# A hybrid decoder layer on one core: the first branch's output projection as seven half-size products per pair of output blocks, with its sums made earlier

## The chip, the cores and the metric

The kernel runs on one core of one Trainium2 chip. The metric is the device time of one execution in microseconds (us); three executions of a kernel make its median. One profiled execution has a time of its own and a trace. The engines are TensorE (PE, with its weight loads shown apart as PEld), VectorE (DVE), ScalarE (ACT), GpSimd (POOL) and SyncE (SP), whose queue issues the DMA transfers.

## The reference

One layer with two token mixers, x of shape 1024 tokens by 1024 columns, all in float32 (D = 1024):

```
h = RMSNorm(x);  proj = h @ w_in               # all queries, keys, values, gates, merge logits
# branch a: gated linear attention (GLA), 4 heads, dk 128, dv 256, chunks of 64
o_gla = rmsnorm(gla_chunked(q, k, v, log_a), gla_norm_g) * silu(g_gate)
y_a = o_gla @ w_pa                             # "the first branch's output projection"
# branch b: stick-breaking attention, 8 heads, d 128, strictly causal
o_sb = stick_breaking(q, k, v) * silu(s_gate)
y_b = o_sb @ w_pb
g = sigmoid(m_logits + b_gate)                 # one gate per branch and column
x = x + (g_a * y_a + g_b * y_b) @ w_o
return rmsnorm(x) * final_g
```

## The kernel before, in words

**Products.** A float32 matrix product is made of three matmuls: each operand is split into a high part (ACT copies it rounded) and a low part (DVE subtracts the high part), and high x high, high x low and low x high are added in one PSUM bank. `split` does one such pair; its ACT and DVE halves stand at lines 164 and 165. Matmuls have 128 rows of weights and up to 512 columns; T = 1024 tokens are two halves of 512.

**The seven-product form.** The big projections work on pairs of blocks: two blocks of 128 output columns by two halves of tokens, with the 1024 inner rows in two interleaved sets (even and odd blocks of 128). The four quarter matrices on each side, A11 to A22 and B11 to B22, are replaced by seven products of half-size operands, which need sums of quarters: S1 to S4 of the activations and T1 to T4 of the weights. One product is 4 inner blocks x 3 = 12 matmuls of 128x512; a direct pair of output blocks takes 8 x 12. `pair_job` does this for the input projection, with units 0 to 6, and three PSUM banks in turn (tag pp; x, y and z are three of its uses). In each job POOL makes the weight sums (lines 243 to 246) and DVE and ACT empty the banks (lines 275 and 308).

**Stages**, by the profile's time: norm and first values to 103 us; 31 pair jobs from 103 to 770; stick-breaking attention from 770 to 990; the rest of branch a's projection to 1015; branch b's and the output projection, both in the seven-product form, to the end.

Beside the pair jobs other work is placed by hand: `djobs` (decay factors of GLA, the first 25 units), `tjobs` (T sums of w_pb and w_o on DVE, line 839, loaded and stored by DMA), and then the GLA recurrence, 32 steps of (head h, block b of 128 tokens), each with four units of pair jobs: `gl_local` and `gl_out` make the attention of a block, `gl_gate` transposes the normed output of the step before, multiplies it by its gate g (line 973), splits the result and stores it as high and low parts in `d_ogl`. In `gl_out`, r = 1/rms goes DVE - POOL (line 230) - DVE (line 963).

The stick-breaking stage has 64 steps of (head h, block i): `scores` (matmuls z, sigmoid on ACT, a scan on DVE, line 1074), `turn` (transposes on PE, line 1086, splits by ACT and DVE into ath, atl, afh, afl) and per half head `values` (matmuls av, lines 1107 to 1109, then a multiply on DVE, line 1112, and a store to `d_osb`, line 1114). PE gets filler units between them: `st = Line(line)` is a list of loads and units, and `st.run(n)` does the next n units with the loads ahead of them. `SB_PLAN` says how many units stand at each step. The filler is four last gate products and branch a's output projection: `pa(eb, n)`, one output block of 128 columns by one half of the tokens, 24 matmuls (`proj_t`, lines 203 to 205), whose result is multiplied by the merge gate (`ma_half`, line 1162) and stored in `d_ma`.

After the stage, branch b starts: `a_load` brings the stored attention outputs (line 1258), `o_split` splits them (`o_hi` on ACT, line 1306, `o_lo` on DVE, line 1310), and the first products go to tile xa (line 1361). The last units of the filler are placed between these splits. From here on the instructions of ACT, DVE and PE keep the order of the code in the region under `manual_schedule`; elsewhere a scheduler orders them.

## Time and profile before

| | |
|---|---|
| median of 3 executions | 1176.99 us (1176.26 to 1654.08) |
| profiled execution, its own time | 1176.68 us |
| its span in the trace | 1175.0 us |
| PE busy | 1162.1 us, 99% |
| weight loads (PEld) busy | 979.5 us, 83% |
| DVE busy | 857.2 us, 73% |
| ACT busy | 558.3 us, 48% |
| POOL busy | 244.3 us, 21% |
| memory read / written | 150.06 MB / 88.08 MB |

Busy time is the union of an engine's instructions; the span runs from the first to the last event of the trace. Groups of instructions are written as "line engine operation out<-in", with the program's names of tiles. A DVE row "f<-pp,f" reads PSUM bank pp and tile f and writes f. An entry such as [2.00 <-DMA A<-d_osb] behind a row is the time for which the engine stood idle ahead of it and what ended that time.

### The profile page before, as it was taken

The page shows a single profiled execution, that of the slowest core. Times are in us where ns is not written, and L with a number is a line of the kernel's source. Part 1 is how long each engine was busy: PE and PEld are TensorE (multiplying, and loading weights), DVE is VectorE, ACT ScalarE, POOL GpSimd, SP SyncE. Part 2 cuts the span into 40 slices and gives each one's busy share as a digit, 9 for nine tenths or more (in the row PEclk, how much of TensorE's full clock was granted, in tenths as well). Part 3 has the DMA queues.
Part 4 walks back from the last instruction along what each step waited for, and adds up shares of the span by engine and source line. Part 5 has one row for each costly group of instructions (what it writes and reads, how often), then busy time and mean ns, then how long its engine had stood idle before and what let it go on. Part 6 is the DMA issues. An engine that isn't in the chain of part 4 may idle for free.

```text
span 1175.0 us, 16650 instructions
## 1 busy us (share of the span) xinstructions
PE 1162.1 (99%) x5823; PEld 979.5 (83%) x5823; DVE 857.2 (73%) x1441; ACT 558.3 (48%) x1046; POOL 244.3 (21%) x217
## 2 busy tenths in 40 slices
PE   8999999999999999999999999999999999999997
PEld 8999888887888888888888888888888888888886
DVE  6797667888676876776666677457677876488986
ACT  6556663433444545544444343344444444365544
POOL 1022232334242242342242233000000000700001
PEclk9999999999999999999999999999999999999999
DMA  8325549997455665654444357799766656858652
GB/s 290 127 63 162 206 165 327 329 308 241 134 185 180 195 217 162 201 178 133 159 141 131 109 174 237 260 311 337 250 200 216 205 167 195 284 162 286 215 197 108
DMA packets 189456, 239.25 MB, mean 204 GB/s; under 512 B 12438, under 2 KB 128300, under 8 KB 187836
## 3 DMA queue, kind: packets, MB, share of 16 engines
q1 hardware_dynamic: 188796, 237.20, 61.1%
...
q14 instruction: 38, 0.31, 0.1%
HBM read 150.06 MB, written 88.08 MB: 203 GB/s over the span
## 4 chain that ended last, share of the span: by engine, by line
PE 96%; DVE 2%; DMA 1%; ACT 1%; issue 1%; SPq 0%; POOLq 0%; POOL 0%; ACTq 0%; DVEq 0%
PE pp L269 17%; PE pp L270 17%; PE pp L271 17%; PE pp L204 3%; PE pp L205 3%; PE pp L203 3%; PE pp L222 2%; PE av L1108 2%; PE av L1109 2%; PE tr L1086 1%; PE av L1107 1%; PE z L1068 1%; PE z L1070 1%; PE z L1069 1%; PE xa L1363 1%; PE xa L1362 1%
## 5 line engine op out<-in xcount | busy, mean ns | idle before, releaser
L269 PE MATMUL pp<-S,wh 128*128 128x512 f32 x372 | 147.0, 395 | 0.7 <-ACT f L275 0.7
L271 PE MATMUL pp<-S,wl 128*128 128x512 f32 x372 | 145.0, 390 | 0.0
L270 PE MATMUL pp<-S,wh 128*128 128x512 f32 x372 | 144.9, 390 | 0.0
L308 DVE TENSOR_TENSOR f<-pp,f 128x512 f32<-128x512 f32 x93 | 63.9, 687 | 70.2 <-PE pp L271 63.8
L165 DVE TENSOR_TENSOR wl<-tt,wh 128x1024 fp32r<-128x1024 f32 x62 | 75.8, 1222 | 52.6 <-ACT wh L164 52.3
L164 ACT ACTIVATE wh<-tt 128x1024 fp32r<-128x1024 f32 x62 | 65.6, 1059 | 75.0 <-PE pp L270 67.4
L243 POOL TENSOR_TENSOR tt<-raw 128x512 f32<-128x512 f32 x31 | 43.5, 1403 | 258.8 <-DVE wl L165 232.8
L275 ACT ACTIVATE f<-pp 128x512 f32<-128x512 f32 x93 | 55.0, 592 | 79.8 <-PE pp L271 74.2
L1074 DVE TENSOR_TENSOR_SCAN be<-be,m 128x128 f32<-128x128 f32 (+3 forms) x64 | 86.1, 1347 | 3.4 <-ACT be L1071 3.2
L164 ACT ACTIVATE wh<-raw 128x1024 fp32r<-128x1024 f32 (+1 forms) x47 | 48.4, 1030 | 84.0 <-PE pp L270 48.5
L269 PEld LDWEIGHTS pp<-S,wh 128*128 128x128 f32 x372 | 70.5, 190 | 15.1 <-ACT f L275 0.9
L271 PEld LDWEIGHTS pp<-S,wl 128*128 128x128 f32 x372 | 69.8, 188 | 14.8
L270 PEld LDWEIGHTS pp<-S,wh 128*128 128x128 f32 x372 | 69.9, 188 | 13.8
L165 DVE TENSOR_TENSOR wl<-raw,wh 128x1024 fp32r<-128x1024 f32 (+1 forms) x47 | 63.1, 1343 | 18.4 <-ACT wh L164 17.2
L1071 ACT ACTIVATE be<-z 128x384 f32<-128x384 f32 (+4 forms) x96 | 47.2, 494 | 42.7 <-PE z L1070 38.2
L230 POOL TENSOR_TENSOR r<-r,nhalf 128x1 f32<-128x1 f32 x40 | 25.2, 629 | 194.3 <-DVE r L229 194.3
L1268 POOL TENSOR_TENSOR N<-A,A 128x512 f32<-128x512 f32 x4 | 6.6, 1660 | 241.0 <-DMA A<-d_osb 241.0
L269 PE MATMUL pp<-ha11h,wh 128*128 128x512 f32 x124 | 49.2, 397 | 0.0
L269 PE MATMUL pp<-ha12h,wh 128*128 128x512 f32 x124 | 49.0, 395 | 0.0
L164 ACT ACTIVATE dh<-raw 128x512 fp32r<-128x512 f32 x31 | 19.6, 631 | 61.4 <-PE pp L270 61.4
L269 PE MATMUL pp<-ha22h,wh 128*128 128x512 f32 x124 | 48.7, 393 | 0.0
L269 PE MATMUL pp<-S,dh 128*128 128x512 f32 x124 | 48.6, 392 | 0.0
...
## 6 DMA issues: line engine op xcount, KB each, us to landing
...
```

The costliest lines, as they stand in the source:

```text
L164: nc.scalar.activation(hi, src, AF.Copy)
L165: eng.tensor_sub(lo, src, hi.bitcast(F32))
L203: nc.tensor.matmul(pt, whi[:, kb], h_, start=kb == 0, stop=False)
L204: nc.tensor.matmul(pt, whi[:, kb], l_, start=False, stop=False)
L243: nc.gpsimd.tensor_sub(t1, b[:, 0, 1], b[:, 0, 0])
L269: nc.tensor.matmul(pt, bh[:, j], ah[:, j], start=first and j == 0, stop=False, skip_group_check=True)
L270: nc.tensor.matmul(pt, bh[:, j], al[:, j], start=False, stop=False, skip_group_check=True)
L271: nc.tensor.matmul(pt, bl[:, j], ah[:, j], start=False, stop=j == 3, skip_group_check=True)
L275: nc.scalar.activation(t[nm], t[bank], AF.Copy)
L308: nc.vector.tensor_add(add, bank, add)
L1071: nc.scalar.activation(om[:, off + pc * w:off + (pc + 1) * w], zt[:, 0:w], AF.Sigmoid, scale=-inv_sqrt)
L1074: nc.vector.tensor_tensor_scan(rest, rest, m1[:, off:T][:, ::-1], 1.0, op0=ALU.mult, op1=ALU.max)
```

## The change

Branch a's output projection takes the seven-product form. For each of 4 pairs of output blocks, i = 0 to 3, there are seven products of 12 matmuls: 28 x 12 = 336 in place of 16 x 24 = 384. They are grouped into units: A(i) with A11 B11 and S2 T2, B(i) with A12 B21, C(i) with S1 T1 and S4 B22, and D with S3 T3 and then A22 T4 for two values of i, added to one bank. A, B and C are filler of the stick-breaking stage; D is done after it. Between units, partial results u and w are kept in memory (`d_u`, `d_w`).

The sums are made earlier. The T sums of w_pa are made on DVE beside the decays (`tp_load`, `tp_sum`, `tp_store`, into `d_tp`). The S sums of the GLA output are made in `gl_gate`: for b < 4 (the first half of the tokens) the gated block is also stored in `d_g0`; for b >= 4 it is loaded again as gp, POOL makes four 128x128 sums of g and gp, and two more splits and two stores put them into `d_os`. g and gp are loaded in the middle of a step (`gl_g`) instead of two steps ahead. The mask tri moves to another tile. The tail is written in another order: `o_split("bA11")` ahead of the first unit instead of behind it, under `manual_schedule` from there on.

```diff
-SB_PLAN = [0, 0, 0, 1, 0, 0, 1, 0]
+PA_PLAN = {**{(h, 6): 2 if h == 5 else 1 for h in range(8)}, **{(h, 3): 1 for h in (0, 1, 2, 4, 6)}}
...
+    TSUMS = ((0, 1, 0), (1, 3, 1), (3, 3, 0), (2, 2, 3))
+    def tp_load(j):
+        tp[j] = dq.tile([P, 4, HALF], F32, tag="tp", name="tp")
+        for two in range(2):
+            rows = slice((2 * j + two) * P, (2 * j + two + 1) * P)
+            for e in range(2):
+                nc.sync.dma_start(tp[j][:, 2 * two + e].rearrange("p (i c) -> p i c", c=P),
+                                  w_pa[rows].rearrange("p (i e c) -> p e i c", e=2, c=P)[:, e])
+    def tp_sum(j, i):
+        dst, x1, x2_ = TSUMS[i]
+        nc.vector.tensor_sub(tp[j][:, dst], tp[j][:, x1], tp[j][:, x2_])
+    def tp_store(j):
+        nc.sync.dma_start(d_tp[:, j], tp.pop(j))
...
+    for j, (load_at, *sums_at, store_at) in enumerate(((0, 3, 4, 5), (6, 8, 10, 11), (12, 15, 17, 18), (19, 22, 23, 24))):
...
-    for jobs in djobs:
+    for k, jobs in enumerate(djobs):
         pairs.run(1, *jobs)
+        for fn, args in pjobs.get(k, ()):
+            fn(*args)
...
-    tri = gv.tile([P, P], F32, tag="tri", name="tri", bufs=1)
+    tri = const.tile([P, P], F32, tag="rcode", name="tri")
...
-        g = gv.tile([P, 2, P], F32, tag="g", name="g", bufs=3)
-        nc.sync.dma_start(g, d_gg[h][:, :, b * P:(b + 1) * P])
+    def gl_g(h, b):
+        for nm, src, b_ in (("g", d_gg, b), ("gp", d_g0, b - 4))[:1 + b // 4]:
+            g = gblk[h, b][nm] = gv.tile([P, 2, P], F32, tag="g", name="g", bufs=4)
+            nc.sync.dma_start(g, src[h][:, :, b_ * P:(b_ + 1) * P])
...
+        if b < 4:
+            nc.sync.dma_start(d_g0[h][:, :, b * P:(b + 1) * P], t["g"])
+            return
+        g, gp = t["g"], t["gp"]
+        for dst, x1, x2_, fn in ((g[:, 1], g[:, 0], g[:, 1], ALU.add), (g[:, 0], gp[:, 0], g[:, 0], ALU.subtract),
+                                 (gp[:, 0], g[:, 1], gp[:, 0], ALU.subtract),
+                                 (gp[:, 1], gp[:, 1], gp[:, 0], ALU.subtract)):
+            nc.gpsimd.tensor_tensor(dst, x1, x2_, op=fn)
+        o = stage().rearrange("p e (s c) -> p e s c", c=P)
+        for i, src in enumerate((g, gp)):
+            split(src, *(o[:, e, 2 * i:2 * i + 2] for e in range(2)))
+        for e in range(2):
+            nc.sync.dma_start(d_os[:, :, e, h, (b - 4) * P:(b - 3) * P], o[:, e].bitcast(F32))
...
-        pairs.run(4)
+        pairs.run(2)
+        gl_g(h, b)
+        pairs.run(2)
...
+    def pa_mm(a, b, i, pt=None):
...
+        for j in range(4):
+            nc.tensor.matmul(pt, bh[:, j, cs], ah[:, j], start=first and j == 0, stop=False, skip_group_check=True)
+            nc.tensor.matmul(pt, bh[:, j, cs], al[:, j], start=False, stop=False, skip_group_check=True)
+            nc.tensor.matmul(pt, bl[:, j, cs], ah[:, j], start=False, stop=j == 3, skip_group_check=True)
+        return pt
+    def out_put(J, n, i, pt, add, gate_, res):
+        eb = 2 * i + J
+        tc.keep_in_program_order(nc.scalar.activation(gate_, gate_, AF.Sigmoid, bias=vcol[:, eb:eb + 1]))
+        nc.vector.tensor_add(res, pt, add)
+        nc.vector.tensor_mul(res, res, gate_)
+        nc.sync.dma_start(d_ma[eb][:, half(n)], res)
+    def pa_a(i):
+        pt = pa_mm("A11", "B11", i)
+        ps1[i] = f_tile()
+        nc.scalar.activation(ps1[i], pt, AF.Copy)
+        pt, u = pa_mm("S2", "T2", i), f_tile()
+        nc.vector.tensor_add(u, pt, ps1[i])
+        nc.sync.dma_start(d_u[i][:], u)
...
+    def pa_d(i0, J):
+        for i in (i0, i0 + 1):
+            d = pd[i]
+            if J:
+                d["pt"] = pa_mm("S3", "T3", i)
+            else:
+                pa_mm("A22", "T4", i, d["pt"])
+            out_put(J, 1, i, d["pt"], d["wu"[1 - J]], d["o"][:, J], d["wu"[1 - J]])
...
+            C[0], o_dma("A22"), C[1], wload("B22", 1), wload("T3", 0), C[2], C[3], wload("T4", 0),
+            wload("T3", 1), pd_load(0), pd_load(1)]
...
+    wlast = wq_dma("T4", 1, wlast)
+    st = Line([unit_of(pa_d, 0, 1), (lambda: wq_split("T4", 1, wlast), False), pd_load(2), unit_of(pa_d, 0, 0),
+               pd_load(3), unit_of(pa_d, 2, 1), unit_of(pa_d, 2, 0)])
...
+    manual = ExitStack()
+    manual.enter_context(tc.manual_schedule(engines={mybir.EngineType.Activation, mybir.EngineType.DVE,
+                                                     mybir.EngineType.PE}))
+    o_split("bA11", ALL)
     st.run(1)
-    o_split("bA11", ALL)
     o_split("bB11", AB)
...
     sums("b", range(3), ("S1", "S3", "S2"), nc.gpsimd)
-    st.run(1)
     o_load("bT2", "tt")
```

**Order in the recurrence.** POOL's queue at one step with b >= 4 (r is the rms chain, tt the weight sums of a pair job, q2 a part of the next queries), before:

```order
L230 TENSOR_TENSOR r_4598<-r_4598,nhalf_196 128x1
L230 TENSOR_TENSOR r_4743<-r_4743,nhalf_196 128x1
L896 TENSOR_TENSOR q2_5147<-qe_5146,fac_4606 128x512
L243 TENSOR_TENSOR tt_4546<-raw_4544 128x512
L245 TENSOR_TENSOR tt_4546<-raw_4544 128x512
L244 TENSOR_TENSOR tt_4546<-raw_4544,tt_4546 128x512
L246 TENSOR_TENSOR tt_4546<-raw_4544,tt_4546 128x512
```

and with the change, at the same step (g_4632 and g_4634 are g and gp):

```order
L234 TENSOR_TENSOR r_4710<-r_4710,nhalf_210 128x1
L1020 TENSOR_TENSOR g_4632<-g_4632 128x128
L1020 TENSOR_TENSOR g_4632<-g_4634,g_4632 128x128
L234 TENSOR_TENSOR r_4868<-r_4868,nhalf_210 128x1
L1020 TENSOR_TENSOR g_4634<-g_4632,g_4634 128x128
L1020 TENSOR_TENSOR g_4634<-g_4634 128x128
L926 TENSOR_TENSOR q2_5307<-qe_5306,fac_4716 128x512
```

Two sums stand ahead of that step's r, and two behind it. DVE's queue there, before (on is the normed output, asl and the others the splits of the next step):

```order
L229 TENSOR_SCALAR r_4743<-ssq_4741 128x1
L919 TENSOR_TENSOR am1_2639<-pa_4751,tri_2635 64x64
L920 TENSOR_TENSOR am1_2639<-pa_4751,tri_2635 128x64
L963 TENSOR_SCALAR on_4740<-po_4728,r_4743 128x256
L165 TENSOR_TENSOR asl_4757<-am1_2639,ash_4756 128x128
L165 TENSOR_TENSOR vl_4761<-vr_4602,vh_4760 128x256
L165 TENSOR_TENSOR qsl_4765<-q2_4039,qsh_4764 128x128
L165 TENSOR_TENSOR dl_4769<-raw_4347,dh_4768 128x512
```

and with the change:

```order
L233 TENSOR_SCALAR r_4868<-ssq_4866 128x1
L953 TENSOR_TENSOR am1_2693<-pa_4874,tri_2689 64x64
L954 TENSOR_TENSOR am1_2693<-pa_4874,tri_2689 128x64
L997 TENSOR_SCALAR on_4865<-po_4853,r_4868 128x256
L169 TENSOR_TENSOR o_4842<-g_4632,o_4842 128x256
L169 TENSOR_TENSOR o_4842<-g_4634,o_4842 128x256
L169 TENSOR_TENSOR asl_4880<-am1_2693,ash_4879 128x128
L169 TENSOR_TENSOR vl_4884<-vr_4714,vh_4883 128x256
```

Two 128x256 splits of the sums stand between on and asl.

**Order on SP around the last attention values.** d_osb_115 is the store of the last values, A the loads of stored attention outputs, of which the first four are A11; before:

```order
L1155 DMA o<-d_ga_144 128x512
L1258 DMA A_9935<-d_osb_108 128x512
L1258 DMA A_9937<-d_osb_110 128x512
L1114 DMA d_osb_115<-f 128x512
L1258 DMA A_9939<-d_osb_112 128x512
L1258 DMA A_9941<-d_osb_114 128x512
L1258 DMA A_9948<-d_osb_109 128x512
```

and with the change:

```order
L1224 DMA wlast<-d_tp 128x4x256
L1163 DMA d_osb_115<-f 128x512
L1396 DMA A_10284<-d_osb_108 128x512
L1396 DMA A_10286<-d_osb_110 128x512
L1396 DMA A_10288<-d_osb_112 128x512
L1396 DMA A_10290<-d_osb_114 128x512
L1396 DMA A_10297<-d_osb_109 128x512
```

The two A11 loads that stood ahead of the store now stand behind it, and the load of wlast stands there.

**Order on DVE and PE from there.** DVE's queue from the last values on (line 1112, now 1161), before:

```order
L1112 SCALAR_TENSOR_TENSOR f<-av,vend,f 128x128 x4
L1310 TENSOR_TENSOR bB11l<-raw,bB11h 128x1024 x2
L1162 TENSOR_TENSOR o<-pp,o 128x512
L1310 TENSOR_TENSOR bA11l<-A_9935,bA11h 128x512
L1310 TENSOR_TENSOR bA11l<-A_9937,bA11h 128x512
L1310 TENSOR_TENSOR bA11l<-A_9939,bA11h 128x512
L1310 TENSOR_TENSOR bA11l<-A_9941,bA11h 128x512
L1310 TENSOR_TENSOR bA12l<-A_9948,bA12h 128x512
```

and with the change (L1275 and L1276 are the two DVE instructions of `out_put`):

```order
L1161 SCALAR_TENSOR_TENSOR f<-av,vend,f 128x128 x4
L1448 TENSOR_TENSOR bA11l<-A_10284,bA11h 128x512
L1448 TENSOR_TENSOR bA11l<-A_10286,bA11h 128x512
L1448 TENSOR_TENSOR bA11l<-A_10288,bA11h 128x512
L1448 TENSOR_TENSOR bA11l<-A_10290,bA11h 128x512
L1275 TENSOR_TENSOR f<-pp,f 128x512
L1276 TENSOR_TENSOR f<-f,o 128x512
L1275 TENSOR_TENSOR f<-pp,f 128x512
```

All four low halves of A11 stand ahead of the first instruction that empties a bank. PE's queue from the last matmul of the values on, with the change (three rows of one inner block read the high and low parts; pp_10329 is the bank of D for i = 0):

```order
L1158 MATMUL av_10239<-ath_7978,v_9775 128x256
L1254 MATMUL pp_10346<-oa22h_8850,wh_9833 128x512
L1255 MATMUL pp_10346<-oa22l_8851,wh_9833 128x512
L1256 MATMUL pp_10346<-oa22h_8850,wl_9834 128x512
L1254 MATMUL pp_10346<-oa22h_8850,wh_9833 128x512
L1255 MATMUL pp_10346<-oa22l_8851,wh_9833 128x512
L1256 MATMUL pp_10346<-oa22h_8850,wl_9834 128x512
L1254 MATMUL pp_10346<-oa22h_8850,wh_9833 128x512
L1255 MATMUL pp_10346<-oa22l_8851,wh_9833 128x512
L1256 MATMUL pp_10346<-oa22h_8850,wl_9834 128x512
L1254 MATMUL pp_10329<-oa21h_9657,wh_10187 128x512
L1255 MATMUL pp_10329<-oa21l_9658,wh_10187 128x512
```

The rows on pp_10346 are the last nine matmuls of S3 T3. The first on pp_10329 is that of A22 T4, which adds to the bank that L1275 reads first. Before, PE had 112 matmuls of `pa` between the values and the first on xa; it now has 81.

More of the change, by code (lines that the diff above doesn't have):

```diff
@@ L1195, in hybrid_layer, with wq_dma @@
-    for eb in range(5):
-        line += ([pa(eb, 0)] if eb > 2 else []) + [pa(eb, 1), pa_load(eb + 3)]
-    line += [pa(eb, n) for n in range(2) for eb in range(5, KB)]
+    wo = {}
+    def wq_dma(nm, ii, raw):
+        raw = raw.rearrange("p k c -> p (k c)").rearrange("p (j c) -> p j c", j=4)
+        if nm[0] == "T":
+            nc.sync.dma_start(raw, d_tp[:, :, ("T1", "T3", "T4", "T2").index(nm), ii * DV:(ii + 1) * DV])
+        else:
+            e, J = int(nm[1]) - 1, int(nm[2]) - 1
+            rows = w_pa.rearrange("(j e p) c -> e p j c", e=2, p=P)[e]
+            for i in range(2):
+                c0 = (2 * (2 * ii + i) + J) * P
+                nc.sync.dma_start(raw[:, :, i * P:(i + 1) * P], rows[:, :, c0:c0 + P])
+        return raw
@@ L1212, in hybrid_layer @@
             scores(*steps[s + 2])
-        st.run(SB_PLAN[i] if i == 6 or h in (0, 1, 2, 4, 6) else 0)
+        st.run(PA_PLAN.get((h, i), 0))
         turn(h, i)
@@ L1341, in hybrid_layer @@
     o_load("bT3")
-    st.run()
+    st.run(1)
     def part_of(w, j, cols):
```

102 lines of the change are left out of this document (73 added, 29 removed).

## The prediction

> **What bounds the kernel now.** I read the page first (share of each engine, then the chain of work that ended last), then the waits of TensorE (PE), then the stages one by one.
>
> ```profile
> PE 1162.1 (99%) x5823; PEld 979.5 (83%) x5823; DVE 857.2 (73%) x1441; ACT 558.3 (48%) x1046; POOL 244.3 (21%) x217
> PE 96%; DVE 2%; DMA 1%; ACT 1%; issue 1%; SPq 0%; POOLq 0%; POOL 0%; ACTq 0%; DVEq 0%
> ```
>
> PE is busy 99% of 1175.0 us and carries 96% of the chain. The waits of PE (line, what it waited for, us in total, times, longest) say the same: only start-up costs over 1 us.
>
> ```profile
> PE warm L148 <- POOL ident masks.py:199: 1.4, 1, 1.4
> PE pp L222 <- DVE vw L499: 1.3, 1, 1.3
> PE pp L269 <- ACT f L275: 0.7, 1, 0.7
> ```
>
> So a removed matmul is worth its full step as long as nothing else comes late, and a wait that is added on PE counts in full. The step has to be read with care: a row gives 0.39 to 0.40 us, but matmuls overlap. Here are the last matmul of the attention values (its end, 990.05, is called T below), the first two filler matmuls behind it, and the first of the second branch.
>
> ```profile
> 989.77 0.28 PE L1109 MATMUL av<-ath,v 128*128 128x256 f32 x1
> 989.89 0.40 PE L205 MATMUL pp<-oa11h,wl 128*128 128x512 f32 x1
> 990.12 0.40 PE L203 MATMUL pp<-oa12h,wh 128*128 128x512 f32 x1
> 1015.30 0.39 PE L1361 MATMUL xa<-bA11h,bB11h 128*128 128x512 f32 x1
> ```
>
> 112 matmuls stand between the values and the second branch, and (1015.30 - 989.89) / 112 = 0.227 us a step.
>
> **The change part by part.** (1) *Removed matmuls.* The projection had 16 products of 24 matmuls, 384; it now has 4 pairs of 7 products of 12, 336. 48 x 0.227 = **-10.9 us**. By the row's 0.39 it would be -18.7, which no step from start to start supports. In program order 17 of the 48 go before T (-3.9) and 31 after it: the tail goes from 112 to 81 matmuls.
>
> (2) *A new wait in the tail.* Splitting the second branch's A11 used to stand behind a filler unit and now stands before the next one. The rows of SyncE's queue (SPq), ACT and DVE around T:
>
> ```profile
> 988.41 0.91 SPq L1258 DMA_DIRECT2D A<-d_osb  x2
> 991.24 0.32 SPq L1114 DMA_DIRECT2D d_osb<-f  x1
> 991.61 8.10 SPq L1258 DMA_DIRECT2D A<-d_osb  x12
> 995.38 0.63 ACT L1306 ACTIVATE bA11h<-A 128x512 fp32r<-128x512 f32 x1 [2.00 <-DMA A<-d_osb]
> 996.24 0.63 ACT L1306 ACTIVATE bA11h<-A 128x512 fp32r<-128x512 f32 x1 [0.23 <-DMA A<-d_osb]
> 990.09 1.12 DVE L1112 SCALAR_TENSOR_TENSOR f<-av,vend,f 128x128 f32<-128x128 f32 x4 [5.00 <-PE av L1109]
> 993.74 0.69 DVE L1162 TENSOR_TENSOR o<-pp,o 128x512 f32<-128x512 f32 x1 [0.26 <-PE pp L205]
> 996.90 0.69 DVE L1310 TENSOR_TENSOR bA11l<-A,bA11h 128x512 fp32r<-128x512 f32 x1 [0.17 <-ACT bA11h L1306]
> ```
>
> Before, two of the four A11 loads went out at 988.4, ahead of the store that waits for the last values; the other two left from 991.61 and were split at 995.38 and 996.24, while PE had products to go on with. Now all four stand behind that store, so the first leaves at about 991.6, is split from about 995.4, and the fourth comes three spacings later: 3 x 0.45 by the issue (0.91 for two) or 3 x 0.86 by the arrivals (996.24 - 995.38), so 996.7 to 998.0. Add 0.63 on ACT and 0.69 on DVE for the low half, and 0.69 for the eviction that is queued right behind it on DVE: 998.7 to 1000.0. That eviction empties the bank to which PE's tenth matmul after T adds. PE has nine matmuls until then, 9 x 0.227 = 2.0 us, to 992.1. It then stands for 6.6 to 7.9 us; I take **+7.2**. The tail so has 81 x 0.227 = 18.4 of work and 7.2 of waiting, 25.6 against 25.4 before: its gain is gone. What is behind is covered: until it has emptied the next bank, DVE has three 128x1024 splits (wlast, bB11) and four evictions to do, 3 x 1.23 + 4 x 0.69 = 6.5 us by the rows of term 4, and PE has 36 matmuls (8.2 us) to go on with.
>
> (3) *The clock after that wait.* Windows at the end of the span (PE, weight loads, DVE, ACT, POOL busy, granted clock, DMA):
>
> ```profile
> 1167.65 0.28 PE L1490 MATMUL pp<-wT4h,A22l 128*128 128x256 f32 x1
> 1170.00:1171.00 1.00, 0.00 (x0) 0.00 (x0) 0.56 (x2) 0.30 (x1) 0.66 (x1) 1.00 0.40 154
> 1171.00:1172.00 1.00, 0.00 (x0) 0.00 (x0) 0.25 (x1) 0.31 (x1) 0.00 (x0) 0.59 0.00 0
> 1172.00:1173.00 1.00, 0.00 (x0) 0.00 (x0) 0.00 (x0) 0.00 (x0) 0.00 (x0) 0.50 0.89 344
> ```
>
> PE's last matmul ends at 1167.93, and the granted clock falls to 0.50 between 1171 and 1172, about 3.3 us later. A stall of 7 us is longer than that, so PE should resume at half clock. How long it stays there no row of before shows: at least 0, at most all 72 matmuls left, which would lose another 16.3. I take as long as the fall needed, 3.3 us at half speed, which loses 1.65: **+1.7**. The Trainium skill, "TensorE: Matmul & The Clock Gate", section "What's actually happening", gives about 3.4 us of activity until the full clock returns; an estimate by it is a loss of 1.7, and no run here shows it yet.
>
> (4) *More work on DVE in the stick-breaking stage.* Between its first scan and T, DVE gets 13 more filler evictions (26 for 13) and 5 more weight splits (12 for 7).
>
> ```profile
> 770.00:990.00 220.00, 219.53 (x1210) 186.93 (x1209) 161.29 (x242) 102.77 (x218) 0.00 (x0) 1.00 0.70 233
> L165 DVE TENSOR_TENSOR wl<-raw,wh 128x1024 fp32r<-128x1024 f32 x7 | 8.6, 1226 | 6.6 <-ACT wh L164 6.0
> L1162 DVE TENSOR_TENSOR o<-pp,o 128x512 f32<-128x512 f32 x11 | 7.6, 692 | 28.2 <-issue 16.1 <-PE pp L205 12.1
> PEld tr L1086 <- DVE atl L165: 5.6, 17, 0.5
> ```
>
> That is 13 x 0.69 + 5 x 1.23 = 15.1 us on an engine that had 220 - 161.3 = 58.7 free, so on average it is covered, and PE loses only 3.9 us of cover. But weight loads of the transposes already wait 17 times for a DVE split, 5.6 us in all. Between 0 and 15.1 I take **+1.0**, near the lower end, because the free time is four times the addition.
>
> (5) *The recurrence.* In 16 of its 32 steps POOL makes four 128x128 sums, two of them ahead of r, for which DVE waits; DVE and ACT then split two more 128x256 tiles. POOL rows of 128x128 don't exist: they lie between r (128x1) and 128x512, 0.55 to 1.3.
>
> ```profile
> 503.29 0.55 POOL L230 TENSOR_TENSOR r<-r,nhalf 128x1 f32<-128x1 f32 x1
> 389.24 1.29 POOL L243 TENSOR_TENSOR tt<-raw 128x512 f32<-128x512 f32 x1 [3.32 <-DVE wl L165]
> 386.56 0.42 DVE L165 TENSOR_TENSOR vl<-vr,vh 128x256 fp32r<-128x256 f32 x1
> 501.00 1.19 DVE L165 TENSOR_TENSOR vl<-vr,vh 128x256 fp32r<-128x256 f32 x1
> 503.88 0.48 DVE L963 TENSOR_SCALAR on<-po,r 128x256 f32<-128x256 f32 x1 [1.69 <-POOL r L230]
> 513.55 0.39 PE L269 MATMUL pp<-S,dh 128*128 128x512 f32 x1
> 514.67 0.68 DVE L308 TENSOR_TENSOR f<-pp,f 128x512 f32<-128x512 f32 x1
> 516.27 0.39 PE L269 MATMUL pp<-ha22h,wh 128*128 128x512 f32 x1
> L308 DVE TENSOR_TENSOR f<-pp,f 128x512 f32<-128x512 f32 x54 | 37.2, 688 | 46.2 <-PE pp L271 43.5 <-issue 2.7
> ```
>
> What PE needs is the eviction L308: the bank whose product ends as the next one begins (513.55) must be empty by 516.27, one product of 12 x 0.227 = 2.7 us later. If DVE comes at once, 2.7 - 0.7 = 2.0 us are to spare; at 514.67 it came 1.1 after that and 0.9 were left. Added per step on DVE: 2 x 0.42 of splits, and up to 1.1 to 2.6 of waiting behind two sums. Against that DVE idles 46.2 / 54 = 0.86 us ahead of each eviction. Between nothing and 16 x 1.1 = 18 I take **+2.0**, an overrun of 0.1 a step on average, nearest to the 503.88 row, where 1.69 of waiting for POOL cost PE nothing.
> The Trainium skill, "SBUF — State Buffer", section "Who interferes with whom", speaks against this part: a DVE instruction with two SBUF inputs contends with a GpSimd instruction that reads SBUF. The trace agrees in one pair above: the same 128x256 split took 0.42 alone and 1.19 while POOL made sums.
>
> (6) *Sums beside the decays.* 16 more tensor_sub of 128x512 and 8 MB of transfers:
>
> ```profile
> 200.00:300.00 100.00, 99.31 (x443) 81.39 (x442) 81.19 (x109) 38.19 (x57) 34.42 (x26) 1.00 0.86 285
> L839 DVE TENSOR_TENSOR t<-t x32: 678/692/1783, 190.5 to 270.0; 128x512 f32<-128x512 f32 x32
> ```
>
> 32 such sums (median 0.692 each) in a stretch with DVE at 81% and DMA at 0.86 left PE 99.3 of 100. The new 16 x 0.69 = 11.1 us come earlier, beside the decays. Between 0 and 11.1 I take **+0.4**.
>
> **Sum.** -10.9 + 7.2 + 1.7 + 1.0 + 2.0 + 0.4 = +1.4. Against the profiled run of 1176.68 (span 1175.0 and 1.7 around it; the median 1176.99 is 0.3 higher) that gives **1178**.
>
> **Rivals.** *No stall in the tail.* If the A11 data come early, or PE doesn't wait for that eviction, terms 2 and 3 go: 1178 - 8.9 = 1169. For it: before, the same splits cost PE nothing. Against it: the order on SP, DVE and PE. Chance 0.13. *DVE becomes the bound in the stick-breaking stage.* With half of the 15.1 us on the path, 1178 - 1.0 + 7.5 = 1184.5. For it: 5.6 us of waits for atl already; against it: 58.7 us free. Chance 0.14. *The recurrence goes slower (the other side).* If the contention of the pair 0.42 and 1.19 holds for the new splits, they cost 2 x 1.19 = 2.4 a step, and with two sums of 0.55 to 1.29 ahead of r DVE is 3.5 to 5.0 late. It decides once the delay passes the 2.0 to spare; the overrun of 1.5 to 3.0 in 16 steps is 24 to 48 us, and with 2.0 taken out of the sum the time is 1200 to 1224. For it: the 0.9 left at 514.67. Against it: the 0.86 of idle time ahead of each eviction. Chance 0.07.
>
> **How the numbers follow.** My forecast has 0.66, by itself 1173 to 1183 (stall 6.6 to 7.9, clock 0 to 3.3, the other terms up to twice their value). The range of 1167 to 1189 takes in the first two rivals and leaves out the third and the far ends of terms 3 to 5. Two per cent is 23.5 us, about what a measurement can tell from no change. Faster by that needs under 1153.5, beyond the 10.9 that the matmuls can give: 0.01. Slower needs over 1200.5, the third rival: 0.07. The rest, 0.92, is within.
>
> **What would show it.** Right: 48 matmuls of L205's kind fewer; one PE wait of about 7 us on a DVE eviction some 2 us after the last values, a granted clock of 0.50 behind it, and the second branch starting 25 to 28 us after T; T itself no more than 4 us earlier, minus what terms 4 to 6 take. Wrong: a tail under 20 us, many PE waits on atl, or on L308's evictions in the 16 steps with sums.

## The result: 1205.87 us, 2.5% slower, and the profile after

The median of six executions of the changed kernel is 1205.87 us (1205.05 to 1208.23), against 1177.02 for the kernel before: a ratio of 1.0248, interval 1.0234 to 1.0262. One of the six executions of the kernel before took 1654.08 us; the ratio is of the fast executions alone. The profiled execution has a span of 1203.1 us, 28.1 more than before. The first thing to read is again the share of PE and the chain of work that ended last.

```profile
PE 1158.9 (96%) x5775; PEld 972.1 (81%) x5775; DVE 915.6 (76%) x1519; ACT 576.0 (48%) x1088; POOL 282.2 (23%) x281
PE 72%; issue 6%; DMA 6%; POOL 6%; DVE 6%; ACT 2%; SPq 1%; POOLq 0%; DVEq 0%; ACTq 0%
```

The 48 matmuls are gone (5823 to 5775). But PE, which carried 96% of the chain, now carries 72%; POOL, DMA and DVE have 6% each. The work became less, and the waiting became more. The waits of PE in the whole span (line, what it waited for, us in total, times, longest) name the places:

```profile
PE pp L1254 <- DVE f L1275: 15.3, 2, 11.1
PE pp L273 <- DVE f L312: 4.9, 6, 1.7
PE pp L273 <- ACT f L279: 3.7, 2, 2.2
```

L1254 is the projection's own matmul in the tail, L273 that of the pair jobs; L1275, L312 and L279 empty banks. A list of waits shows neither a slow clock nor many short delays. So I also worked out an **excess** from the start times of all matmul rows: for each neighbouring pair, the time from start to start beyond the usual step of its shape (0.227 us for 512 columns), summed by stage.

| excess of PE, us | before | after | difference |
|---|---|---|---|
| start (to 100 us) | 8.6 | 8.6 | 0.0 |
| decays and T sums of w_pa (100 to 280) | 0.2 | 5.8 | +5.6 |
| recurrence and the other pair jobs (280 to the first z) | 17.7 | 26.4 | +8.7 |
| stick-breaking stage (first z to T) | 11.8 | 16.4 | +4.6 |
| tail and rest (from T) | 0.1 | 19.7 | +19.6 |
| sum | 38.4 | 76.9 | +38.5 |

38.5 - 10.9 for the removed matmuls is 27.6, against 28.1 in the span: the table accounts for the loss. T itself comes 15.0 us later (1005.0 for 990.05; -3.9 + 5.6 + 8.7 + 4.6 = 15.0), and xa starts 37.8 after T where it started 25.3 after.

**The tail.** Rows of the timelines of SP, ACT, DVE and PE from T on (start, duration, engine, line, operation, tiles, count, and in brackets the idle time ahead and what ended it):

```profile
1004.73 0.28 PE L1158 MATMUL av<-ath,v 128*128 128x256 f32 x1
1005.93 0.53 SPq L1224 DMA_DIRECT2D wlast<-d_tp  x1
1007.16 10.66 SPq L1396 DMA_DIRECT2D A<-d_osb  x14
1014.20 2.58 ACT L1444 ACTIVATE bA11h<-A 128x512 fp32r<-128x512 f32 x4 [16.46 <-DMA A<-d_osb]
1014.87 2.64 DVE L1448 TENSOR_TENSOR bA11l<-A,bA11h 128x512 fp32r<-128x512 f32 x4 [8.68 <-ACT bA11h L1444]
1017.42 0.68 DVE L1275 TENSOR_TENSOR f<-pp,f 128x512 f32<-128x512 f32 x1
1018.16 0.79 PE L1254 MATMUL pp<-oa21h,wh 128*128 128x512 f32 x1 [11.08 <-DVE f L1275]
1028.15 6.82 DVE L1448 TENSOR_TENSOR bA12l<-A,bA12h 128x512 fp32r<-128x512 f32 x4
1034.89 0.68 DVE L1275 TENSOR_TENSOR f<-pp,f 128x512 f32<-128x512 f32 x1
1035.71 0.47 PE L1254 MATMUL pp<-oa21h,wh 128*128 128x512 f32 x1 [4.25 <-DVE f L1275]
```

The predicted stall is there: A11 is loaded, split on ACT and DVE, then the bank is emptied, then PE goes on. It lasts 11.08 where 6.6 to 7.9 was forecast, because the data land 7.0 us after the first load's issue (1007.16 to 1014.20, by the start of the split on ACT); before it was 3.8 (991.61 to 995.38). And there is a second stall of 4.25: four splits of A12 take 6.82 us on DVE, 1.7 each, and stand ahead of the third unit's eviction. Before, the same split took 0.63:

```profile
1000.64 1.89 DVE L1310 TENSOR_TENSOR bA12l<-A,bA12h 128x512 fp32r<-128x512 f32 x3
1027.63 1.74 POOL L1406 TENSOR_TENSOR A<-N,A 128x512 f32<-128x512 f32 x1
```

The second row, of the kernel after, is what runs beside them now: POOL's S sums of branch b.

What stands ahead of A11 on SP, in before (the first two rows) and after (the last three):

```profile
976.21 1.89 SPq L1284 DMA_DIRECT2D raw<-in_w_pb_dram  x3
980.95 1.48 SPq L1278 DMA_DIRECT2D tt<-d_t  x3
997.73 1.22 SPq L1422 DMA_DIRECT2D raw<-in_w_pb_dram  x2
1002.62 2.13 SPq L1422 DMA_DIRECT2D raw<-in_w_pb_dram  x3
1004.86 1.03 SPq L1416 DMA_DIRECT2D tt<-d_t  x2
```

Before, these loads of branch b's weights and of its T sums had all been issued by 983.4, 5 us ahead of the first A11 load. Now five loads of weights, two of tt, two of gates and the 512 KB of wlast, 2.75 MB in all, leave in the 9 us before A11. As I read it, the filler's weight splits hold the load buffers longer: the last of them ahead of these loads ends on DVE at 997.63, and the first two loads leave at 997.73.

**The clock.** Windows of the tail (us; busy time of PE, weight loads, DVE, ACT and POOL; granted clock; DMA share; GB/s):

```profile
1008.00:1010.00 2.00, 0.00 (x0) 0.00 (x0) 0.00 (x0) 0.00 (x0) 0.00 (x0) 0.76 0.73 235
1010.00:1012.00 2.00, 0.00 (x0) 0.00 (x0) 0.00 (x0) 0.00 (x0) 0.00 (x0) 0.50 1.03 357
1020.00:1022.00 2.00, 2.00 (x6) 1.58 (x5) 2.00 (x3) 2.00 (x4) 0.22 (x1) 0.50 1.05 394
1022.00:1024.00 2.00, 2.00 (x8) 1.57 (x8) 2.00 (x2) 2.00 (x5) 1.92 (x2) 0.83 1.03 382
1036.00:1038.00 2.00, 2.00 (x7) 1.56 (x6) 1.90 (x3) 2.00 (x5) 1.92 (x3) 0.58 0.92 352
```

PE stopped at 1007.08 (1018.16 - 11.08). A mean clock of 0.76 from 1008 to 1010 puts its fall to half at about 1009.0, 2 us later, and it is still half from 1020 to 1022. At the second stall PE stopped at 1031.46 and went on at 1035.71; by the 0.58 of the last window the clock fell only at about 1036.3. By the starts of the matmuls, the step is 0.427 from 1018.16 to 1022.6 (4.4 us) and again, after the second stall, from 1036.26 to 1039.59 (3.3 us). That loses 7.7 x (1 - 0.227 / 0.427) = 3.6 us. 11.1 + 4.25 + 3.6 = 18.95 of the tail's 19.7.

**The recurrence.** One step with sums, on POOL, ACT and PE:

```profile
495.62 1.12 POOL L1020 TENSOR_TENSOR g<-g 128x128 f32<-128x128 f32 x2 [0.70 <-DVE o L169]
497.22 1.20 POOL L1020 TENSOR_TENSOR g<-g 128x128 f32<-128x128 f32 x2
496.77 0.42 ACT L168 ACTIVATE o<-g 128x256 fp32r<-128x256 f32 x1 [0.86 <-POOL g L1020]
498.45 0.42 ACT L168 ACTIVATE o<-g 128x256 fp32r<-128x256 f32 x1 [1.06 <-POOL g L1020]
499.72 0.58 ACT L279 ACTIVATE f<-pp 128x512 f32<-128x512 f32 x1
500.35 0.50 PE L273 MATMUL pp<-S,dh 128*128 128x512 f32 x1 [1.49 <-ACT f L279]
L1020 POOL TENSOR_TENSOR g<-g 128x128 f32<-128x128 f32 x64 | 34.1, 532 | 71.4 <-DVE o L169 64.1
```

A sum of 128x128 takes 0.53 on POOL on average. ACT stands 0.86 and 1.06 for them, since its splits of the sums come next in its line. Behind them in the same line, after one more weight split, stands L279, which empties a bank, and PE waits 1.49 for it.

This isn't one step alone. The groups of these splits over the whole stage, on ACT before (the first row) and after, and on DVE after:

```profile
L164 ACT ACTIVATE o<-g 128x256 fp32r<-128x256 f32 x32 | 13.0, 406 | 1.5 <-DVE g L973 0.7 <-ACT qsh L164 0.5 <-DMA d_k<-o 0.3
L168 ACT ACTIVATE o<-g 128x256 fp32r<-128x256 f32 x64 | 26.3, 412 | 46.2 <-POOL g L1020 40.8 <-DMA d_k<-o 1.9 <-DVE g L1007 1.5
L169 DVE TENSOR_TENSOR o<-g,o 128x256 fp32r<-128x256 f32 x64 | 35.0, 548 | 13.6 <-ACT o L168 13.1
```

ACT stands 46.2 us ahead of them, 40.8 of it for POOL's sums, where it stood 1.5 before; DVE stands 13.6, nearly all for ACT's half of the same split, where it stood 0.4. The splits themselves didn't get longer on DVE: 0.55 on average, for 0.61 before.

**The decays.** DVE and PE at two places:

```profile
153.60 0.69 DVE L831 TENSOR_TENSOR tp<-tp 128x512 f32<-128x512 f32 x1 [1.45 <-DMA tp<-in_w_pa_dram]
158.81 1.39 DVE L831 TENSOR_TENSOR tp<-tp 128x512 f32<-128x512 f32 x2
161.25 0.68 DVE L312 TENSOR_TENSOR f<-pp,f 128x512 f32<-128x512 f32 x1
161.99 0.50 PE L273 MATMUL pp<-ha22h,wh 128*128 128x512 f32 x1 [1.72 <-DVE f L312]
187.78 0.69 DVE L555 SCALAR_TENSOR_TENSOR f<-f 128x512 f32<-128x512 f32 x1 [1.79 <-DMA f<-d_e]
190.98 0.47 PE L273 MATMUL pp<-S,wh 128*128 128x512 f32 x1 [1.50 <-DVE f L555]
```

DVE stands 1.45 for the weights that the new sums read. From there DVE has next to no pause until 161.93. At the end of this stretch two more sums and a weight split stand ahead of an eviction, and PE waits 1.72. And DVE stands 1.79 for a transfer of decay factors (f<-d_e).

### The profile page after: what moved, and what is told of

It is laid out like the page before. It is cut to its first block, busy times and chain, and to the rows that moved or that the text cites. A ratio compares the mean times of both kernels' runs of the same rounds, so it can differ in the third digit from the quotient of the medians.

```text
span 1203.1 us, 17066 instructions
## 1 busy us (share of the span) xinstructions
PE 1158.9 (96%) x5775; PEld 972.1 (81%) x5775; DVE 915.6 (76%) x1519; ACT 576.0 (48%) x1088; POOL 282.2 (23%) x281
## 4 chain that ended last, share of the span: by engine, by line
PE 72%; issue 6%; DMA 6%; POOL 6%; DVE 6%; ACT 2%; SPq 1%; POOLq 0%; DVEq 0%; ACTq 0%
PE pp L273 12%; PE pp L274 12%; PE pp L275 12%; POOL g L1020 2%; PE pp L226 2%; PE pp L1254 1%; PE pp L1255 1%; PE pp L1256 1%; PE av L1156 1%; PE av L1158 1%; PE av L1157 1%; PE xa L1502 1%; PE xa L1501 1%; PE xa L1503 1%; PE xb L1625 1%
## 5 line engine op out<-in xcount | busy, mean ns | idle before, releaser
L273 PE MATMUL pp<-S,wh 128*128 128x512 f32 x372 | 147.4, 396 | 1.5 <-DVE f L555 1.5
L169 DVE TENSOR_TENSOR wl<-tt,wh 128x1024 fp32r<-128x1024 f32 x62 | 76.9, 1240 | 35.1 <-ACT wh L168 34.6
L312 DVE TENSOR_TENSOR f<-pp,f 128x512 f32<-128x512 f32 x93 | 63.7, 686 | 51.1 <-PE pp L275 46.4
L168 ACT ACTIVATE wh<-raw 128x1024 fp32r<-128x1024 f32 (+1 forms) x52 | 53.6, 1031 | 73.4 <-PE pp L274 31.3
L279 ACT ACTIVATE f<-pp 128x512 f32<-128x512 f32 x93 | 54.7, 590 | 65.2 <-PE pp L275 61.6
L169 DVE TENSOR_TENSOR wl<-raw,wh 128x1024 fp32r<-128x1024 f32 (+1 forms) x52 | 71.3, 1372 | 18.0 <-ACT wh L168 15.9
L273 PEld LDWEIGHTS pp<-S,wh 128*128 128x128 f32 x372 | 70.6, 190 | 16.6 <-ACT wh L168 1.9
L275 PEld LDWEIGHTS pp<-S,wl 128*128 128x128 f32 x372 | 69.9, 188 | 14.9
L273 PE MATMUL pp<-ha22h,wh 128*128 128x512 f32 x124 | 49.4, 399 | 4.9 <-DVE f L312 4.9
L273 PE MATMUL pp<-S,dh 128*128 128x512 f32 x124 | 48.9, 394 | 3.7 <-ACT f L279 3.7
L1020 POOL TENSOR_TENSOR g<-g 128x128 f32<-128x128 f32 x64 | 34.1, 532 | 71.4 <-DVE o L169 64.1
L273 PE MATMUL pp<-ha11h,wh 128*128 128x512 f32 x124 | 49.2, 397 | 0.0
L273 PE MATMUL pp<-ha12h,wh 128*128 128x512 f32 x124 | 49.0, 395 | 0.0
```

The costliest lines, as they stand in the source:

```text
L168: nc.scalar.activation(hi, src, AF.Copy)
L169: eng.tensor_sub(lo, src, hi.bitcast(F32))
L273: nc.tensor.matmul(pt, bh[:, j], ah[:, j], start=first and j == 0, stop=False, skip_group_check=True)
L275: nc.tensor.matmul(pt, bl[:, j], ah[:, j], start=False, stop=j == 3, skip_group_check=True)
L279: nc.scalar.activation(t[nm], t[bank], AF.Copy)
L312: nc.vector.tensor_add(add, bank, add)
```

## The experiments

Ratios are to the kernel before, run beside each; "excess" is the table's number for a stage, of the profiled run. No version here is faster than before. The excess of a stage isn't the same in all runs that leave that stage as the change has it: the decays have 4.9 to 7.9 (a wait at the border of 280 us falls to one side or the other), the recurrence 26.4 to 28.2, the stick-breaking stage 15.3 to 16.4 (17.8 in e6) and the tail 19.3 to 21.1. One or two microseconds of excess in a single run therefore show nothing.

Five of the sixteen times (e2, e5, e7, e15, e16) lie where the theory under test put them. e6, e9, e11, e12, e13 and e17 came out slower than anything that was expected of them.

### The tail

**e1_tail**: the units are done earlier, two ahead of the splits of A11 and one more ahead of the splits of B11, so that the evictions of their banks no longer stand behind these.

```diff
+    st.run(1)
+    st.run(1)
     o_split("bA11", ALL)
-    st.run(1)
-    o_split("bB11", AB)
...
+    st.run(1)
+    o_split("bB11", AB)
     sums("b", range(3), ("S1", "S3", "S2"), nc.gpsimd)
...
     o_load("bT1")
-    st.run(1)
     o_split("bB21", AB)
...
     o_load("bT3")
-    st.run(1)
```

> The tail in another order: both products of the first D pair come before the splits of A11, the split of B11 stands between the other two D units, and POOL's sums and the A12 splits come behind. Nothing else differs from the changed kernel (1205.9). Theory 'in line' (evictions queued on DVE behind splits whose data are late): both PE waits (11.1 and 4.25 us) and the half clock behind them (about 3.6 us) go, a new wait of up to 2 us ahead of the second branch: 1187 to 1190. Rival 'the loads are the bound' (the A11 data arrive 9 us after the last values whatever the order, and the second branch can't start earlier): PE only waits elsewhere, ahead of xa, and the time stays at 1202 to 1206.

Measured: 1201.24 us, 1.0208 (1.0193 to 1.0223). The tail's excess goes from 19.7 to 15.3 only. Waits of PE from 1003 us on, and the row of DVE behind the longest:

```profile
PE pp L1254 <- DVE f L1275: 8.2, 2, 6.2
1026.65 0.69 DVE L1275 TENSOR_TENSOR f<-pp,f 128x512 f32<-128x512 f32 x1 [3.82 <-DMA f<-d_w]
```

The eviction isn't behind the splits any more, yet PE waits for the same line: it now needs f<-d_w, the partial result w, whose load stands behind the A loads on SP. One wait has taken the place of another.

**e16_a12_behind**: only the split of A12 is moved behind the third unit.

```diff
-    o_split("bA12", ALL)
     sums("b", [3], ("S1", "S3", "S2"), nc.gpsimd)
     o_load("bT1")
     st.run(1)
+    o_split("bA12", ALL)
```

> The changed kernel with one move: the splits of A12 stand behind the third D unit's evictions instead of ahead of them. Theory 'in line' (the A12 splits, slowed by POOL's sums beside them, hold up the eviction): the second wait of 4.25 us and the half clock behind it (about 1.5 us) go, 1200 to 1202. Rival (the eviction's other operand, w of the third pair, is late too): the wait only changes its cause, 1204 to 1206.

Measured: 1201.09 us, 1.021 (1.0192 to 1.0228). The place of the second stall on PE:

```profile
1036.10 0.50 PE L1254 MATMUL pp<-oa21h,wh 128*128 128x512 f32 x1 [0.82 <-DVE f L1275]
```

The second wait falls from 4.25 to 0.82, the tail's excess from 19.7 to 14.1, and the time by 4.8. So the second stall, with its spell of half clock, is due to the place of these four splits. They are as long at their new place (6.90 us for the four, for 6.82), but no eviction that PE waits for stands behind them.

**e14_no_wpb**: 3 MB of branch b's weights (B11, B21, T2) are not loaded but filled with a constant by POOL; the order on ACT, DVE and PE stays, and A11 keeps its place behind the store.

```diff
+        if nm in ("bB11", "bB21", "bT2"):
+            for j in range(4):
+                nc.gpsimd.memset(raw[:, j], 0.5)
+            return
```

> The changed kernel without the loads of three weight operands of the second branch (bB11, bB21, bT2: twelve of 256 KB around the last values; POOL fills the tiles with a constant in their place, so that part of the computation is left out). The loads of A11 keep their place in the queue, behind the store of the last values. Theory 'bytes ahead': A11 is split 3.4 to 4.5 us after its first issue in place of 7.0, PE's long wait falls from 11.1 to 7 to 8.5 us, the second wait shrinks too: 1196 to 1202. Rival 'place behind the store': the wait stays at 10 to 11.5, 1203 to 1206.

Measured: 1202.64 us, 1.0211 (1.0195 to 1.0228); the tail's excess is 16.7. SP, ACT and PE:

```profile
1005.88 8.11 SPq L1396 DMA_DIRECT2D A<-d_osb  x14
1009.63 0.63 ACT L1448 ACTIVATE bA11h<-A 128x512 fp32r<-128x512 f32 x1 [12.57 <-DMA A<-d_osb]
1014.35 0.80 PE L1254 MATMUL pp<-oa21h,wh 128*128 128x512 f32 x1 [7.96 <-DVE f L1275]
```

Without those transfers A11 lands 3.75 us after its issue, as before the change, and PE waits 7.96. So 8.0 of the 11.1 remain without these transfers, close to the prediction's upper end of 7.9, and the transfers give 3.1. That the 8.0 comes from the place behind the store is the prediction's working and was not tested by itself.

**e10_extra_1mb** tried the reverse: four copies of 256 KB within memory were put ahead of A11.

```diff
     wlast = wq_dma("T4", 1, wlast)
+    for i in range(4):
+        nc.sync.dma_start(d_x[i][:], d_osb[SB_H - 1][:, half(0)])
```

> The changed kernel with 1 MB of additional transfers (four copies of 256 KB from memory to memory, which nobody waits for), issued some 7 us before the last values. Theory 'bytes' (the transfer engines are full around the end of the stick-breaking stage, and A11 lands when what stands ahead of it is done): the long wait of PE grows from 11.1 to 13 to 15 us, 1208 to 1211. Rival 'order and latency' (A11 lands a fixed time after its issue, which the store of the last values sets): 11 to 11.5 us and 1205 to 1207.

Measured: 1205.59 us, 1.0239 (1.0224 to 1.0255), tail's excess 19.2, longest wait 9.5. The time lies where the rival had it, but this is inconclusive. The copies pushed other loads (two of w_pb, two of tt) out of the 9 us ahead of A11, so that again 2.75 MB left there, and the run doesn't add what it was to add.

**e6_tail_need** issues the loads in the order of need: A12 behind the second unit, A21 and A22 behind the third, all sums behind the fourth, and splits wlast only ahead of the last unit.

```diff
-               pd_load(3), unit_of(pa_d, 2, 1), unit_of(pa_d, 2, 0)])
+               pd_load(3), unit_of(pa_d, 2, 1), (lambda: wq_split("T4", 1, wlast), False), unit_of(pa_d, 2, 0)])
...
-    a_load("A12", ALL)
-    a_load("A21", range(3))
-    a_load("A22", range(3))
...
+    st.run(1)
+    st.run(1)
     o_split("bA11", ALL)
+    a_load("A12", ALL)
     st.run(1)
...
```

> The tail with transfers and splits in the order of need: evictions ahead of all splits as in the tail kernel above (1201.2), and besides the loads of A12, A21 and A22 are issued behind the loads of w and u for the last two pairs, and the split of wlast stands only ahead of the unit that uses it. Theory 'late data in line' (the tail waits for wlast, w and u, which stand behind 14 other loads): the waits of 2.0 and 6.2 us that the tail kernel still has go, less 1 to 3 us of new waits for A12 later: 1191 to 1196. Rival 'bytes' (the transfer engines are full in the tail, over 1.0 by the windows, and the sum of bytes sets the start of the second branch): 1199 to 1203.

Measured: 1207.58 us, 1.026 (1.0239 to 1.028), the tail's excess 21.6: no gain.

```profile
PE pp L1501 <- DVE kept L1538: 8.8, 1, 8.8
PE pp L1254 <- ACT wh L168: 5.9, 1, 5.9
```

PE now waits 5.9 for the high half of the last weights, on ACT, and 8.8 in branch b, where POOL's sums come late.

**e11_d_later** loads A11 and B11 ahead of wlast and does branch b's first four products between the second and the third unit, as cover.

```diff
     a_load("A11", ALL)
     o_load("bB11")
+    wlast = mo.tile([P, KB, P], F32, tag="wr", name="wlast")
+    wlast = wq_dma("T4", 1, wlast)
...
+    st.run(2)
     o_split("bA11", ALL)
...
+    for it in items[:4]:
+        a_product(*it)
+    late_tail()
```

> The tail with less in front of A11 and more cover behind it: the loads of A11 are issued ahead of wlast, PE does the first pair of D units at once, then the first four products of the second branch, and only then the other D units, whose data have the 11 us of those products longer to arrive. Theory 'bytes' (the data come at the rate of the transfers, and only other work on PE helps): the tail's PE waiting and half clock of 20 us fall to 6 to 12, 1191 to 1199. Rival (the waits only move again, to the products that need A12 and POOL's sums): 1201 to 1207.

Measured: 1209.21 us, 1.027 (1.0253 to 1.0287), tail's excess 23.5. xa starts 12.4 after T, as meant, but it was no cover:

```profile
PE pp L1503 <- DVE bB21l L1444: 5.6, 1, 5.6
PE xa L1501 <- ACT bB11h L1440: 4.9, 1, 4.9
```

Whichever operand PE is given first, it waits for that one. In the three windows of the changed kernel above that lie between 1010 and 1024, the DMA share is 1.03 to 1.05 at 357 to 394 GB/s. As I read it, all that the tail loads after T competes, and a new order only chooses what is late.

### The recurrence

**e2_gla_nosum** leaves out POOL's four sums; the splits and stores stay. **e3_gla_dve** makes them on DVE. **e7_late_split** leaves them on POOL but does their splits and stores half a step later.

```diff
-            nc.gpsimd.tensor_tensor(dst, x1, x2_, op=fn)
+            nc.vector.tensor_tensor(dst, x1, x2_, op=fn)
```

This is e3; e2 leaves out the whole loop. And e7:

```diff
+        pend.append((g, gp, h, b))
...
+    def gl_flush():
+        while pend:
+            g, gp, h, b = pend.pop()
+            o = stage().rearrange("p e (s c) -> p e s c", c=P)
+            for i, src in enumerate((g, gp)):
+                split(src, *(o[:, e, 2 * i:2 * i + 2] for e in range(2)))
...
         pairs.run(2)
+        gl_flush()
         gl_g(h, b)
```

> The recurrence without the four POOL sums per step: the splits take g and gp as they are (part of the computation left out), all loads, splits and stores stay. Theory 'in line' (ACT and DVE stand in the queue for POOL's sums, and evictions of the pair jobs behind them come late): the stages of the recurrence lose 7 to 9 us of PE waiting, 1197 to 1199. Rival 'more work' (two more splits on ACT and DVE and two more loads and stores per step): nothing comes back, 1204 to 1206.

> The same four sums per step, made on DVE in place of POOL. Theory 'in line': no wait between engines, 4 x 0.28 us more on DVE in 16 steps, which has idle time: PE waits of the recurrence fall from 8.7 to 1 to 3 us, 1198 to 1201. Rival 'more work': DVE has 1.1 us more per step, PE waits more, 1206 to 1215.

> POOL's sums in the recurrence stay, but the splits and stores of their results stand half a step later, so that ACT and DVE find them ready. Theory 'in line' (it is the wait for POOL, not the work of the sums or splits): as without the sums, 1198 to 1200. Rival 'shared memory port' (POOL's sums slow DVE's own splits wherever they stand): 1203 to 1206.

| | time, us | ratio (interval) | excess of the recurrence, us |
|---|---|---|---|
| the change | 1205.87 | 1.0248 (1.0234 to 1.0262) | 26.4 |
| e2, no sums | 1198.3 | 1.0173 (1.0156 to 1.019) | 19.8 |
| e3, sums on DVE | 1201.92 | 1.022 (1.0205 to 1.0235) | 23.5 |
| e7, splits later | 1198.1 | 1.0178 (1.0163 to 1.0193) | 18.3 |

e7 does all the work of the change, with the same sums on POOL, and its recurrence is 8.1 us better, down to 0.6 above the kernel before. That is as much as leaving the sums out brings. So neither the sums nor the splits are too much work; ACT and DVE stood in line for POOL with evictions behind them. In e7 ACT stands 20.8 us for POOL ahead of these splits, for 40.8, and DVE 3.2, for 13.6. DVE's splits are even longer there, 0.63 on average for 0.55, so their length isn't what costs. With the sums on DVE the gain is 2.9: DVE's standing goes as well (1.5), but ACT still stands 13.2 for the sums, and their work is added on DVE.

### The decays

**e5_notp** leaves out the loads, sums and stores of the T sums of w_pa and reads the T sums of w_pb in their place. **e8_tp_late** has the loads of the last three groups one job earlier and the first sums of the second and third group one job later. **e12_late_tppool** makes the sums on POOL, on top of e7.

```diff
-        for fn, args in pjobs.get(k, ()):
-            fn(*args)
```

```diff
-    for j, (load_at, *sums_at, store_at) in enumerate(((0, 3, 4, 5), (6, 8, 10, 11), (12, 15, 17, 18), (19, 22, 23, 24))):
+    for j, (load_at, *sums_at, store_at) in enumerate(((0, 3, 4, 5), (5, 9, 10, 11), (11, 16, 17, 18), (18, 22, 23, 24))):
```

```diff
-        nc.vector.tensor_sub(tp[j][:, dst], tp[j][:, x1], tp[j][:, x2_])
+        nc.gpsimd.tensor_sub(tp[j][:, dst], tp[j][:, x1], tp[j][:, x2_])
```

> Without the sums of w_pa beside the decays: no loads, sums or stores there; the T operands are read from the stored sums of w_pb instead (part of the computation left out). If these sums and their transfers cause all PE waiting between 100 and 300 us (4.5 us in three places): 1201 to 1202. Rival (the pair jobs' new order in that stage causes it): 1205 to 1206.

> The loads of w_pa for the second to fourth group of sums go out one unit earlier and the sums of the second and third stand one unit later. If DVE's wait for these loads is the cause in the stage of the decays: one of the three waits (1.7 us) goes, 1203 to 1205. If the transfers themselves delay the decay factors (the wait of 1.5 on f<-d_e), that wait stays or grows: 1205 to 1207.

> The splits of the recurrence's sums half a step later (as in the kernel of 1198.1) and the sums of w_pa beside the decays on POOL in place of DVE, with the same transfers. If DVE's line (its wait for the w_pa data and three sums ahead of an eviction) is the cause in the decays: the waiting of 5.8 us there falls to 1.5 to 3, 1194 to 1196. If the transfers are (late decay factors): it stays, 1197 to 1200.

e5: 1201.9 us, 1.0215 (1.0194 to 1.0235); the excess of the decays is 0.1, so the T sums and their transfers cost all 5.6 us there. e8: 1205.57, 1.0251 (1.0228 to 1.0274), 6.8: the shift by one job gains nothing. e12: 1214.92, 1.0323 (1.0308 to 1.0339). Its recurrence keeps e7's gain in the main (19.7), but the decays lose 23.0. Waits of PE from 100 to 285 us:

```profile
PE pp L275 <- DVE wl L169: 7.8, 1, 7.8
```

POOL makes the pair jobs' own weight sums; the new ones stand in their line, and PE waits 7.8 at once for a weight split.

### The stick-breaking stage

**e17_mul_pool** moves the 16 gate multiplications of `out_put` from DVE to POOL, to see whether DVE's added work is what the stage lost.

```diff
-        nc.vector.tensor_mul(res, res, gate_)
+        nc.gpsimd.tensor_mul(res, res, gate_)
```

> The gate multiplication of the projection's 16 outputs on POOL in place of DVE, nothing else. Eight stand in the stick-breaking stage, where POOL is idle: 5.5 us less on DVE there. If DVE's additional work causes that stage's extra 4 us of PE waiting, 1.5 to 3 of them go: 1203 to 1205 (and the tail may gain one or two more). If single late transfers cause it (q, the gate of values), nothing goes: 1205 to 1207.

Measured: 1214.76 us, 1.0313 (1.0296 to 1.033). The stage's excess is 15.8, and it is 15.3 to 15.9 in all but one of the other versions, none of which touches this stage; so e17 brings nothing back there that can be told from their spread. The loss is in the tail (26.4), where POOL's L1276 becomes late itself:

```profile
L1276 POOL TENSOR_TENSOR f<-f,o 128x512 f32<-128x512 f32 x8 | 12.0, 1514 | 18.4 <-DMA A<-d_osb 18.4
```

So the eight multiplications in the stage, 5.5 us of DVE's work, are not what it lost. DVE's other added work there, evictions and weight splits, was not taken away in any run. Where the loss lies can be read from PE's waits in this stage, before (the first row) and after:

```profile
PE tr L1086 <- DVE atl L165: 0.2, 1, 0.2
PE tr L1135 <- DVE atl L169: 2.1, 5, 0.6
PE z L1117 <- DMA q<-d_q: 0.9, 1, 0.9
PE av L1156 <- DVE f L1161: 0.8, 1, 0.8
```

They grow from 0.2 to 3.8 us, most of the 4.6, and fall in seven places: five transposes wait for a split on DVE, one matmul for the load of q, and one for a bank that DVE empties right behind a scan of 2.28 us. What makes these seven late stays open.

### Several at once

**e9_all** is e6, e7 and e8 together; **e13_all2** is e11 and e12; **e15_tail_late** is e1 and e7.

> The three mends together (tail in the order of need, splits half a step later, sums of w_pa later). If the parts are independent, as the theory of separate queues has it, their gains add up: 1205.9 less 10 to 15 for the tail, 6 to 8 for the recurrence, 1 to 3 for the decays: 1181 to 1188. Rival (each gain is taken by the next late thing): 1190 to 1196.

> The last two together: D units later, splits of the sums half a step later, sums of w_pa on POOL. If the three parts are independent their gains add up: 1180 to 1188. Below 1177 only if the tail loses nearly all its waiting, which the bytes speak against.

> The two mends that gained, together: evictions of the tail ahead of the A11 splits (1201.2 alone) and the splits of the recurrence's sums half a step later (1198.1 alone). Independent parts: 1205.9 - 4.7 - 7.8 = 1193.4, so 1192 to 1195. Rival (the tail's gain was partly that of another order in the recurrence): 1196 to 1199.

| | time, us | ratio (interval) | excess: decays, recurrence, stick-breaking, tail |
|---|---|---|---|
| e9 | 1198.66 | 1.018 (1.0162 to 1.0199) | 5.9, 18.2, 15.6, 19.6 |
| e13 | 1218.55 | 1.0351 (1.0336 to 1.0367) | 22.6, 19.5, 15.4, 24.0 |
| e15 | 1192.0 | 1.0128 (1.011 to 1.0146) | 5.2, 18.8, 15.7, 15.0 |

The parts add: e1 gained 4.63 and e7 7.77, so that 1205.87 - 12.4 = 1193.5, and e15 takes 1192.0. The 1.5 us between may be a spell of half clock near 410 us, which e1 has and e15 hasn't (see the last section). It is the fastest changed version, still 1.3% slower than before. What it still pays over the kernel before is 14.9 in the tail, 5.0 in the decays, 3.9 in the stick-breaking stage and 1.1 in the recurrence, against 10.9 saved on matmuls.

## Why the prediction was wrong

It gave 1178 (1167 to 1189) and the time is 1205.87. It is 27.9 short, and each step past the first has a part in it:

| step | predicted | measured | by |
|---|---|---|---|
| (1) removed matmuls | -10.9 | -10.9 | 48 fewer, and the table closes with 0.227 a step |
| (2) a new wait in the tail | +7.2 | +15.3 | 11.08 and 4.25 |
| (3) the clock after it | +1.7 | +3.6 | two spells at half speed |
| (4) more work on DVE in the stick-breaking stage | +1.0 | +4.6 | excess 11.8 to 16.4 |
| (5) the recurrence | +2.0 | +8.7 | excess 17.7 to 26.4 |
| (6) sums beside the decays | +0.4 | +5.6 | excess 0.2 to 5.8 |

*Step 2*: the mechanism was right, its place to the matmul. Two claims failed. That "the first leaves at about 991.6, is split from about 995.4" took over a landing time of 3.8 from the row of before, but what stood ahead of that row on the queue had changed; e14 gives back 3.1 by taking those transfers away. And "What is behind is covered" counted three splits and four evictions and left out the four splits of A12, which stand ahead of an eviction too; e16 shows them to be worth 4.8 us. They were also 2.7 times as long as before (1.70 for 0.63), beside POOL's sums.

*Step 3*: the first spell lost 2.1 against 1.7; the second came with the second stall, of which the prediction knew nothing. Its delay of 3.3 us from PE's stop to the fall of the clock was no constant either: it was about 2.0 at the first stall and 4.9 at the second, where PE was already going on. The Trainium skill, "TensorE: Matmul & The Clock Gate", section "What's actually happening", gives about 3.4 us of activity until the full clock is back; the spells of 4.4 and 3.3 us bear it out roughly, and the first was longer.

*Step 5* failed in what it counted. It counted DVE's two new splits and DVE's waiting for r behind two sums, set DVE's idle time against them, and took an overrun of 0.1 a step. It left out that the splits of the sums make ACT and DVE themselves stand for POOL, and that ACT empties banks too: of PE's waits for evictions in this stage, 3.7 us are for ACT and 2.4 for DVE. e7 takes back 8.1 of the 8.7 without removing an instruction. The third rival named this stage and 1200 to 1224, and the time lies there, but not by its mechanism: it had the whole loss in the recurrence, by long splits on DVE, and these splits were not longer than before (0.55 for 0.61). That its range holds the time is luck.

*Step 6* failed likewise: "a stretch with DVE at 81%" has room for 11.1 us of work on average. DVE keeps its order, though, so a sum whose data are late, or which stands just ahead of an eviction, holds up what is behind it. e5 shows that the whole 5.6 comes from this part; that it is the waiting in line rather than the work is read from the rows at 153.60 and 161.99, and no run separates them, since e8's other places gained nothing.

*Step 4* had the sign right and 1.0 for 4.6. What failed is its reason, "the free time is four times the addition": PE's named waits in the stage went from 0.2 to 3.8 us all the same, in seven single places. What makes these late is open. The second rival (half of DVE's 15.1 us on the path) would give 7.5; e17, which takes 5.5 us of that work off DVE, brings back nothing beyond the spread of the runs.

Where cover was judged by a share of free time (steps 4 to 6) each term came out at four to fourteen times its estimate.
